# Metering side work to an allowance per weight unit in a two-layer block on one core, with the high parts of both units ahead of both low parts, and another start and end

## The chip, the cores and the metric

One core of one Trainium2 chip runs the whole program. The time is device microseconds (us) of one execution; several executions are timed and the median is given. TensorE (PE) multiplies; VectorE (DVE), ScalarE (ACT) and GpSimd (POOL) do elementwise work; SyncE (SP) issues nearly all DMAs.

## The reference, cut to what matters

Batch 1, 256 tokens, width 2048, all in fp32. Two blocks follow one another:

```
def first_block(x, mem, ...):
    h = rmsnorm(x, mix_norm);  proj = h @ w_mix_in                  # 2048 -> 7184
    y_gdn = gated_delta_rule(...conv, silu, l2norm of proj...)      # 8 heads of 128, chunks of 64,
                                                                    # a triangular solve per chunk
    y_sc  = b_gate * causal_dwconv(c_gate * h)                      # width 1024
    x = x + concat(y_gdn, y_sc) @ w_mix_out
    x = x + softmax(q k^T) v @ w_xo                                 # q from rmsnorm(x), k, v from rmsnorm(mem)
    x = x + (silu(gate) * up) @ w_ffn_down                          # gate, up = causal_dwconv(rmsnorm(x) @ w_ffn_up)
    return rmsnorm(x, final_norm)
def second_block(x, ...):
    proj = rmsnorm(x, g_pre) @ w_in
    o_mla = causal softmax attention, 8 heads, rope, low-rank q and kv;  times silu(gate)
    o_fox = causal softmax attention, 8 heads, with forget gates;        times silu(gate)
    return x + rmsnorm(concat(o_mla, o_fox) @ w_out, g_post)
```

## The kernel before

Every large weight is cut into units of 128 x 1024 (512 KB), 704 in all, which go by in one long list (`stream`). fp32 accuracy comes from two parts of each operand: a high part, rounded to the fast fp32r type, and a low part, the remainder. Unit i is loaded by SP (`load`, L335, 8 units ahead), rounded by ACT (`split_hi`, L342, into the tile `whi`, 3 units ahead, 4 buffers), and its remainder is made by DVE (`split_lo`, L349, into `wlo`, 2 units ahead, 3 buffers).

TensorE then works on the unit's 8 blocks of 128 x 128 (`blocks`): 8 high matmuls 128x512 of `whi` against a token tile that holds high and low part side by side (`x`, 2 x 256 columns), and 8 low matmuls 128x256 of `wlo` against the high part of the token tile alone. Most products (`jobB`) are jobs of two units that sum 16 blocks into one PSUM bank: high (L217) and low (L219) of the first unit, seven high, eight low and one last high (L221) of the second. There are four such banks. A job ends with `merge` (L226, L228), an ACT copy and a DVE add that bring the bank to SBUF and set it free. Products with tokens as the stationary side (`jobA`, L296 to L298: w_xv, w_fv, w_out_2) use three matmuls 128x512 per block and token half. In the last of them both token halves share the weights: some units of the second half are held back (`early`) until the sums of the first half are under way.

All else is side work in Python generators, each of which issues a few instructions and yields: squares of the inputs for the first norm (`g_first`, whose adds on POOL stand at L533 and which PE sums at L412), the gated delta rule (`g_gdn`, `g_base` for the 16x16 triangular bases at L870 and L872), convolutions after the merges (L463, L466), the memory branch (`g_mem`), attention heads (`g_xhead`, `g_head`), output gates (`p_outgate`), and the end (`g_out`). After each unit `step` advances every live generator once, whatever it issues. So the list of units, and how many generators are alive, set the order of instructions on DVE and ACT, where `split_lo` and `split_hi` stand in line with side work:

```
for i, u in enumerate(units):
    self.split_hi(i + self.LOOK_HI)
    self.split_lo(i + self.LOOK_LO)
    for h in hooks.get(id(u), ()):
        h()
    u[2](self.whi.pop(i), self.wlo.pop(i))
    ...
    self.step()
```

At the start SP issues the constants `cst` (259 KB), the first token tiles `xr0` (256 KB), the first unit `raw0` (512 KB), then the other seven token tiles with units between them; `first_x` scales each token tile (L518 on ACT, L519 on DVE) and ten warm-up matmuls on zeros (L505, 20 records in the trace) run ahead of the first weight. At the end `p_last` and `g_out` do for each token half: ACT squares (L1445), a DVE multiply by the gain (L1446), a reciprocal root in small steps, and per half four tiles of o * r + x: three on DVE (L1463) and one on ACT and POOL (L1460, L1461), then four output DMAs on SP.

## Time and profile before

| | us |
|---|---|
| median of 3 runs (lowest, highest) | 2079.64 (2078.51, 2080.05) |
| profiled execution | 2080.9 |
| its span, first to last instruction | 2079.1 |
| PE busy in the span | 2056.3 (99%) |
| DVE busy | 1484.6 (71%) |
| ACT busy | 1096.8 (53%) |
| POOL busy | 184.4 (9%) |

Spans and busy times are of the profiled execution, which took 1.26 us more than the median of the runs. Its mean granted TensorE clock was 0.996 of full speed. A matmul's record overlaps the next one's, since they are pipelined: the distance from one start to the next says how long PE needs for each.

### The profile page before, as it was taken

Reading aid. Unit: us, or ns where it says so; the run is one execution under the profiler, and the core shown is the slowest. Engines: PE = TensorE matmul, PEld = TensorE weight load, DVE = VectorE, ACT = ScalarE, POOL = GpSimd, SP = SyncE. Lnnn points to the kernel's source line nnn. Section 1 sums busy time; section 2 is a strip of 40 time slices with the busy share of each in tenths; the row PEclk is TensorE's granted clock in tenths of the full one; section 3 lists DMA queues with packets and bytes.
Section 4 is the critical chain, followed back from the end, with each engine's and each line's share of the span. In section 5 each row is a group of like instructions: output and inputs, shape, how many; then the busy total and the mean of one; then the engine's idle time right before and its main releaser. Section 6 shows DMA issues by size and latency. Waiting matters only on the chain.

```text
span 2079.1 us, 31159 instructions
## 1 busy us (share of the span) xinstructions
PE 2056.3 (99%) x11734; PEld 1802.6 (87%) x11734; DVE 1484.6 (71%) x2365; ACT 1096.8 (53%) x1751; POOL 184.4 (9%) x174
## 2 busy tenths in 40 slices
PE   8999999999999999999999999999999999999998
PEld 7888898888888898888888888888888888888886
DVE  5988679765467667777775787757779776657855
ACT  5755554644444555465543555434556655546653
POOL 2020012200001001100000000000009430000000
PEclk9999999999999999999999999999999999999999
DMA  7455446545565535555555555555546678544553
GB/s 281 161 174 192 144 152 204 174 152 193 192 225 191 171 112 188 188 189 186 193 185 192 189 187 192 186 189 192 184 156 203 210 217 226 175 157 150 196 185 102
DMA packets 136663, 381.43 MB, mean 183 GB/s; under 512 B 33600, under 2 KB 41536, under 8 KB 136512
## 3 DMA queue, kind: packets, MB, share of 16 engines
q1 hardware_dynamic: 136512, 379.44, 56.0%
q8 instruction: 92, 1.51, 0.3%
q14 instruction: 59, 0.48, 0.1%
HBM read 372.84 MB, written 5.90 MB: 182 GB/s over the span
## 4 chain that ended last, share of the span: by engine, by line
PE 95%; DVE 2%; DMA 1%; ACT 1%; issue 1%; POOL 0%; SPq 0%; DVEq 0%; POOLq 0%; ACTq 0%
PE mm L217 48%; PE mm L219 27%; PE mm L298 4%; PE mm L296 4%; PE mm L297 4%; PE mm L221 3%; DVE wlo L349 1%; POOL acc L533 0%; DMA raw<-w_mix_in 0%; PE ps L399 0%; PE ps L397 0%; PE ps L398 0%; DMA xr<-xT 0%; DVE bt L870 0%; PE ps L1370 0%
## 5 line engine op out<-in xcount | busy, mean ns | idle before, releaser
L217 PE MATMUL mm<-x,whi 128*128 128x512 f32 x4520 | 1153.6, 395 | 3.6 <-ACT whi L342 1.3
L349 DVE TENSOR_TENSOR wlo<-raw,whi 128x1024 fp32r<-128x1024 f32 (+2 forms) x704 | 859.4, 1223 | 386.3 <-PE mm L219 148.4
L217 PEld LDWEIGHTS mm<-x,whi 128*128 128x128 f32 x4520 | 830.1, 189 | 160.1 <-DVE x L519 2.8
L342 ACT CAST whi<-raw 128x1024 fp32r<-128x1024 f32 (+2 forms) x704 | 717.8, 1031 | 259.8 <-PE mm L298 104.0
L219 PEld LDWEIGHTS mm<-x,wlo 128*128 128x128 f32 x4840 | 664.1, 191 | 55.9 <-DVE wlo L349 6.4
L219 PE MATMUL mm<-x,wlo 128*128 128x256 f32 x4840 | 679.3, 283 | 5.2 <-DVE wlo L349 5.2
L226 ACT COPY mg<-mm 128x256 f32<-128x256 f32 x240 | 89.5, 373 | 462.5 <-PE mm L221 462.0
L466 DVE SCALAR_TENSOR_TENSOR cv<-pre,cst,cv 128x256 f32<-128x256 f32 x264 | 130.2, 495 | 9.7 <-ACT cv L463 1.3
L296 PE MATMUL mm<-whi,x 128*128 128x512 f32 x336 | 132.0, 393 | 0.0
L298 PE MATMUL mm<-whi,x 128*128 128x512 f32 x336 | 130.9, 389 | 0.0
L297 PE MATMUL mm<-wlo,x 128*128 128x512 f32 x336 | 130.8, 389 | 0.0
L221 PE MATMUL mm<-x,whi 128*128 128x512 f32 x320 | 126.6, 396 | 0.0
L1134 POOL TENSOR_SCALAR hf<-hf,cst 128x256 f32<-128x256 f32 x16 | 25.2, 1575 | 684.3 <-PE mm L221 683.9
L298 PEld LDWEIGHTS mm<-whi,x 128*128 128x128 f32 x336 | 63.1, 188 | 13.3
L297 PEld LDWEIGHTS mm<-wlo,x 128*128 128x128 f32 x336 | 63.1, 188 | 13.0
L228 DVE TENSOR_TENSOR ms<-mm,mg 128x256 f32<-128x256 f32 x178 | 74.3, 417 | 0.0
L296 PEld LDWEIGHTS mm<-whi,x 128*128 128x128 f32 x336 | 63.1, 188 | 12.7
L221 PEld LDWEIGHTS mm<-x,whi 128*128 128x128 f32 x320 | 61.3, 192 | 0.0
L463 ACT ACTIVATE cv<-pre,cst 128x256 f32<-128x256 f32 x120 | 60.4, 508 | 1.5 <-DVE pre L241 1.5
L447 ACT ACTIVATE x<-hf,cst 128x256 fp32r<-128x256 f32 x32 | 16.4, 513 | 81.1 <-DVE hf L1011 81.1
L241 DVE TENSOR_TENSOR pre<-ms,rb 128x256 f32<-128x256 f32 x112 | 47.6, 428 | 6.0 <-ACT rb L441 2.5
L1116 DVE TENSOR_TENSOR hf<-mm,hf 128x256 f32<-128x256 f32 x48 | 20.2, 421 | 43.2 <-PE mm L221 43.2
(344 smaller groups left out, 1229.2 us busy)
## 6 DMA issues: line engine op xcount, KB each, us to landing
raw<-w_ffn_up SPq DMA_DIRECT2D x176, 512.0 KB, 3.3
raw<-w_mix_in SPq DMA_DIRECT2D x114, 512.0 KB, 3.8
raw<-w_in SPq DMA_DIRECT2D x86, 512.0 KB, 3.4
raw<-w_ffn_down SPq DMA_DIRECT2D x80, 512.0 KB, 3.3
raw<-w_xk SPq DMA_DIRECT2D x32, 512.0 KB, 3.3
raw<-w_xv SPq DMA_DIRECT2D x32, 512.0 KB, 3.3
raw<-w_mix_out SPq DMA_DIRECT2D x32, 512.0 KB, 3.3
raw<-w_xq SPq DMA_DIRECT2D x32, 512.0 KB, 3.3
```

The lines of the kernel that those rows point to most:

```text
L217: T.matmul(ps, hi[:, c[j]], x[j].t, start=first and j == 0, stop=False)
L219: T.matmul(ps[:, 0:TOK], lo[:, c[j]], x[j].hi, start=False, stop=False)
L221: T.matmul(ps, hi[:, c[end]], x[end].t, start=first and end == 0, stop=True)
L226: self.AC.copy(t, ps[:, TOK:])
L228: self.V.tensor_tensor(out, ps[:, 0:TOK], t, ADD)
L296: self.T.matmul(ps, x.hi[:, s], hi[:, c], start=k == 0, stop=False)
L297: self.T.matmul(ps, x.hi[:, s], lo[:, c], start=False, stop=False)
L298: self.T.matmul(ps, x.lo[:, s], hi[:, c], start=False, stop=k == K - 1)
L342: self.AC.copy(hi[:, 0:F], self.raw[i][:, 0:F])
L349: self.V.tensor_tensor(lo[:, 0:F], self.raw.pop(i)[:, 0:F], fl(self.whi[i][:, 0:F]), SUB)
L463: self.AC.activation(t, pre[:, o : o + TOK], AF.Identity, scale=taps[:, 0:1])
L466: self.V.scalar_tensor_tensor(t, pre[:, o + j : o + j + TOK], taps[:, j : j + 1], t, MUL, ADD)
```

## The change

Side work is metered. `Meter` wraps the handles of DVE and ACT that generators use and adds a nominal cost for each instruction issued; the two splits of weights go around it. After each unit `step` adds an allowance (2.1 for DVE, 2.2 for ACT, never saved up), advances new generators first and then the older ones in their order, and stops as soon as either allowance is used up; who was not reached waits for a later unit. A job of two units that is not interleaved with others is "joined": its first unit issues high matmuls alone, its second its high ones, the low ones of both units, and the last high one; for that `wlo` has four buffers. At the start `raw0` is the first load on SP, and ACT issues a small DMA of 8 KB with the norm's gain and `xr0`; `cst` comes after unit 4; the first rounding of weights stands ahead of the token tiles on ACT, two token tiles are rounded on DVE, and there are 6 warm-ups in place of 10. The squares for the first norm are spread over units, half of their sums on DVE. `g_base` yields about twice as often, the memory branch starts at unit 78 in place of 100, and the last `jobA` holds back one unit more. At the end DVE does all four tiles of a half, and the second half's output DMAs alternate between SP and ACT.

```diff
-MEM_AT = 100
-WARM = 10
+MEM_AT = 78
+WARM = 6
+class Meter:
+    COST = {"scalar_tensor_tensor": 0.5, "tensor_tensor": 0.45, "tensor_reduce": 0.4, "activation": 0.45, "copy": 0.45}
+    def __getattr__(self, name):
+        self.spent += self.COST.get(name, 0.2)
+        return getattr(self.eng, name)
+class Job(list):
+    def join(self):
+        self.st["joined"] = len(self) == 2
+        return self
...
+    SPARE = (2.1, 2.2)
...
     def step(self):
-        for g in list(self.gens):
+        m = (self.V, self.AC)
+        for i in range(2):
+            self.left[i] = min(self.left[i] + self.SPARE[i], self.SPARE[i])
+        now, new, self.fresh = self.fresh + self.gens, self.fresh, []
+        self.gens += new
+        for g in now:
+            for i in range(2):
+                self.left[i] -= m[i].spent
+                m[i].spent = 0.0
+            if min(self.left) <= 0:
+                return
             try:
                 next(g)
             except StopIteration:
                 self.gens.remove(g)
-        self.gens += self.fresh
-        self.fresh = []
...
+    def blocks(self, ps, hi, lo, j0, xs, k0, n, first, last, held=()):
+        m = n - 1 if last else n
+        self.highs(ps, hi, j0, xs, k0, m, first)
+        if last:
+            self.need(xs[k0 + m])
+        for h in held:
+            self.lows(ps, *h)
+        self.lows(ps, lo, j0, xs, k0, n)
+        if last:
+            self.T.matmul(ps, hi[:, (j0 + m) * P : (j0 + m + 1) * P], xs[k0 + m].t, start=first and m == 0, stop=True)
...
                 if k0 == 0:
                     st["ps"] = self.mmbank()
-                self.blocks(st["ps"], hi, lo, 0, xs, k0, nk, k0 == 0, k0 + nk == K)
+                    if st["joined"]:
+                        self.highs(st["ps"], hi, 0, xs, 0, nk, True)
+                        st["held"] = [(lo, 0, xs, 0, nk)]
+                        return
+                self.blocks(st["ps"], hi, lo, 0, xs, k0, nk, k0 == 0, k0 + nk == K, st.pop("held", ()))
...
-                if early and n - 1 > i >= n - self.LOOK_LO - 1:
+                if early and n - 1 > i >= n - self.LOOK_LO - 2:
...
-            lo = self._t(self.wp, 1024, "wlo", self.LOOK_LO + 1, "wlo", F32R)
-            self.V.tensor_tensor(lo[:, 0:F], self.raw.pop(i)[:, 0:F], fl(self.whi[i][:, 0:F]), SUB)
+            cuts = [(j * F // parts, (j + 1) * F // parts) for j in range(parts)]
+            lo = self._t(self.wp, 1024, "wlo", self.LOOK_LO + 2, "wlo", F32R)
...
-        nc.sync.dma_start(self.cst, A["cst"])
+        nc.scalar.dma_start(self.mixg, A["cst"][:, 0:KD])
...
+        self.load(0)
+        get(0, nc.scalar)
+        for j in (1, 2, 3):
+            get(j, nc.sync)
...
+            if k in (2, 3):
+                self.V.tensor_scalar(x.hi, src[k], g, None, MUL)
+            else:
+                self.AC.activation(x.hi, src[k], AF.Identity, scale=g)
...
+        for j in range(8):
+            sqs.append(self.S("sq"))
+            self.AC.activation(sqs[j], raws[j], AF.Square)
+            if 0 < j < 4:
+                self.G.tensor_tensor(sqs[0], sqs[0], sqs[j], ADD)
+            if j > 4:
+                self.V.tensor_tensor(sqs[4], sqs[4], sqs[j], ADD)
+            yield
...
-            if spent > 1300:
+            if spent > 700:
...
-            if m == 1:
-                AC.activation(o, o, AF.Identity, scale=r)
-                G.tensor_tensor(o, o, x, ADD)
-            else:
-                V.scalar_tensor_tensor(o, o, r, x, MUL, ADD)
-        for m in (0, 2, 1, 3):
-            self.nc.sync.dma_start(self.A["out"][t * P : (t + 1) * P, m * 512 : (m + 1) * 512], self.og[t, m])
+            V.scalar_tensor_tensor(o, o, r, x, MUL, ADD)
+            q = self.nc.scalar if m % 2 and t else self.nc.sync
+            q.dma_start(self.A["out"][t * P : (t + 1) * P, m * 512 : (m + 1) * 512], o)
```

Three places show how instructions move. The first is TensorE in one job of w_ffn_up. `mm` is the job's PSUM bank, `x` a token tile, `whi` and `wlo` are the unit's two parts. Before, the first unit's low run ends, seven high matmuls of the second unit follow, and its own low run:

```order
L219 MATMUL mm_9199<-x_8361,wlo_9140 128x256
L217 MATMUL mm_9199<-x_8414,whi_9138 128x512
L217 MATMUL mm_9199<-x_8467,whi_9138 128x512
L217 MATMUL mm_9199<-x_8520,whi_9138 128x512
L217 MATMUL mm_9199<-x_8573,whi_9138 128x512
L217 MATMUL mm_9199<-x_8626,whi_9138 128x512
L217 MATMUL mm_9199<-x_8679,whi_9138 128x512
L217 MATMUL mm_9199<-x_8732,whi_9138 128x512
L219 MATMUL mm_9199<-x_8414,wlo_9168 128x256
```

Of the change, the same job at the border of its two units and at the start of its low matmuls:

```order
L250 MATMUL mm_9198<-x_8305,whi_9090 128x512
L250 MATMUL mm_9198<-x_8358,whi_9090 128x512
L250 MATMUL mm_9198<-x_8411,whi_9132 128x512
L250 MATMUL mm_9198<-x_8464,whi_9132 128x512
L250 MATMUL mm_9198<-x_8517,whi_9132 128x512
L250 MATMUL mm_9198<-x_8570,whi_9132 128x512
L250 MATMUL mm_9198<-x_8623,whi_9132 128x512
L250 MATMUL mm_9198<-x_8676,whi_9132 128x512
L250 MATMUL mm_9198<-x_8729,whi_9132 128x512
L254 MATMUL mm_9198<-x_8082,wlo_9134 128x256
L254 MATMUL mm_9198<-x_8102,wlo_9134 128x256
```

The high matmuls of two units now stand in one run of 15, and 16 low ones follow: one change from low to high inside the job is gone, the one at its last high matmul stays. 265 jobs are joined, and 566 places at which a low matmul of a weight is followed by a 128x512 one become 351.

The second place is VectorE at the end of `g_base` in the first group of heads, around the subtractions (L349 before, L403 after) on which TensorE waits. `bt` and `bw` are the scratch of the triangular base, `sch` is a value of the short convolution. Before, the last three row steps of the base stand between two subtractions:

```order
L349 TENSOR_TENSOR wlo_1739<-raw_1462,whi_1706 128x1024
L870 TENSOR_TENSOR bt_356<-bz_354,bw_355 64x169
L872 TENSOR_REDUCE bw_355<-bt_356 64x13
L870 TENSOR_TENSOR bt_356<-bz_354,bw_355 64x196
L872 TENSOR_REDUCE bw_355<-bt_356 64x14
L870 TENSOR_TENSOR bt_356<-bz_354,bw_355 64x225
L872 TENSOR_REDUCE bw_355<-bt_356 64x15
L349 TENSOR_TENSOR wlo_1772<-raw_1515,whi_1737 128x1024
```

Of the change:

```order
L403 TENSOR_TENSOR wlo_2179<-raw_1940,whi_2139 128x1024
L946 TENSOR_TENSOR bt_356<-bz_354,bw_355 64x169
L948 TENSOR_REDUCE bw_355<-bt_356 64x13
L946 TENSOR_TENSOR bt_356<-bz_354,bw_355 64x196
L948 TENSOR_REDUCE bw_355<-bt_356 64x14
L1006 TENSOR_TENSOR x_2137<-scb_1617,x_2137 128x256
L403 TENSOR_TENSOR wlo_2199<-raw_1967,whi_2177 128x1024
L274 TENSOR_TENSOR ms_2227<-mm_2183,mg_2228 128x256
L946 TENSOR_TENSOR bt_356<-bz_354,bw_355 64x225
L948 TENSOR_REDUCE bw_355<-bt_356 64x15
```

The same three steps are now on both sides of a subtraction, and that subtraction is one of a later unit.

The third place is ScalarE in w_out_2, the last weight, where the last head of the second attention (`ps` to `hf`), its gated output (`og`, cast to the token tile `x`) and the rounding of weights share the queue. Before, the copies of the last two heads and both casts stand behind the rounding of `whi_19974` and ahead of the next:

```order
L342 CAST whi_19950<-raw_19719 128x1024
L342 CAST whi_19974<-raw_19755 128x1024
L1374 COPY hf_19992<-ps_19968 128x256
L1374 COPY hf_19992<-ps_19971 128x256
L1420 CAST x_19795<-og_19812 128x256
L1420 CAST x_19869<-og_19886 128x256
L342 CAST whi_19999<-raw_19793 128x1024
```

Of the change, the last head alone, whose tile x_19844 the second of the two blocks of TensorE's unit `whi_19985` reads:

```order
L393 CAST whi_19963<-raw_19748 128x1024
L393 CAST whi_19985<-raw_19774 128x1024
L393 CAST whi_20007<-raw_19822 128x1024
L1441 COPY pT_20025<-ps_20003 128x384
L393 CAST whi_20027<-raw_19842 128x1024
L393 CAST whi_20048<-raw_19886 128x1024
L1452 COPY hf_19957<-ps_20045 128x256
L1498 CAST x_19844<-og_19869 128x256
```

The last head's copy and cast now stand behind the rounding of `whi_20048`, which takes the buffer of `whi_19963`, four units back.

## Rows read from the trace of the kernel before

**Rows 1.** TensorE's waits: what it waited for, us in total, times, longest.

```profile
PE mm L219 <- DVE wlo L349: 5.2, 3, 2.4
PE ps L412 <- POOL acc L533: 2.6, 1, 2.6
...
PE mm L217 <- ACT whi L342: 1.3, 2, 0.7
PE mm L217 <- DVE x L519: 1.2, 2, 1.0
...
PE mm L217 <- DVE x L455: 0.5, 1, 0.5
```

**Rows 2.** Stretches of half clock: busy us per engine, PEclk, DMA share, GB/s.

```profile
12.88:16.29 3.41, 3.41 (x13) 2.97 (x13) 3.41 (x8) 3.41 (x9) 0.00 (x0) 0.50 1.04 410
...
36.77:40.18 3.41, 3.41 (x13) 2.95 (x12) 0.00 (x0) 0.00 (x0) 0.00 (x0) 0.50 1.03 262
...
347.40:350.80 3.40, 3.40 (x10) 2.63 (x9) 3.37 (x5) 1.93 (x3) 1.65 (x1) 0.50 0.84 259
```

**Rows 3.** Timeline of PE after the third long wait: start, us, group.

```profile
347.36 3.58 PE L217 MATMUL mm<-x,whi 128*128 128x512 f32 x8
```

**Rows 4.** Timeline of PE: two job starts, a run of 512, a run of 256.

```profile
1010.27 1.09 PE L217 MATMUL mm<-x,whi 128*128 128x512 f32 x4
...
1038.21 2.00 PE L217 MATMUL mm<-x,whi 128*128 128x512 f32 x8
...
2010.24 0.39 PE L298 MATMUL mm<-whi,x 128*128 128x512 f32 x1
...
2013.87 0.39 PE L296 MATMUL mm<-whi,x 128*128 128x512 f32 x1
...
799.01 0.28 PE L397 MATMUL ps<-pT,th 128*128 128x256 f32 x1
...
801.76 0.28 PE L399 MATMUL ps<-pT,tl 128*128 128x256 f32 x1
```

**Rows 5.** Timeline of the start: ACT, DVE, then PE; in brackets idle before.

```profile
5.09 0.91 ACT L518 ACTIVATE x<-xr,cst 128x256 fp32r<-128x256 f32 x2 [2.85 <-DMA xr<-xT]
7.88 1.05 ACT L342 CAST whi<-raw 128x1024 fp32r<-128x1024 f32 x1 [1.87 <-DMA raw<-w_mix_in]
...
11.31 1.67 DVE L519 SCALAR_TENSOR_TENSOR x<-xr,cst,x 128x256 fp32r<-128x256 f32 x4
...
1.48 6.83 PE L505 MATMUL ps<-zero 128*128 128x256 f32 x20 [1.48 <-DVE zero L502]
8.98 0.73 PE L217 MATMUL mm<-x,whi 128*128 128x512 f32 x2 [0.67 <-ACT whi L342]
...
11.84 1.98 PE L217 MATMUL mm<-x,whi 128*128 128x512 f32 x4 [1.03 <-DVE x L519]
...
15.33 2.45 PE L217 MATMUL mm<-x,whi 128*128 128x512 f32 x8
```

**Rows 6.** Timeline of POOL: the adds of squares for the first norm.

```profile
22.93 12.30 POOL L533 TENSOR_TENSOR acc<-acc,sq 128x512 f32<-128x512 f32 x6 [0.23 <-ACT sq L532]
```

**Rows 7.** Timeline of DVE: two subtractions ahead of the wait at 168.

```profile
161.26 1.22 DVE L349 TENSOR_TENSOR wlo<-raw,whi 128x1024 fp32r<-128x1024 f32 x1
...
166.83 1.21 DVE L349 TENSOR_TENSOR wlo<-raw,whi 128x1024 fp32r<-128x1024 f32 x1
```

**Rows 8.** Timeline of DVE at the end, two groups of the last halves.

```profile
2067.78 3.08 DVE L1463 SCALAR_TENSOR_TENSOR o<-o,ry,xt 128x512 f32<-128x512 f32 x3
2070.79 0.68 DVE L1446 TENSOR_TENSOR o<-mm,gp 128x512 f32<-128x512 f32 x1
```

**Rows 9.** Timeline of the last heads: PE's values, ACT's copies and casts.

```profile
1988.71 0.59 PE L1370 MATMUL ps<-pT,val 128*128 128x256 f32 x2
...
1989.90 0.68 ACT L1374 COPY hf<-ps 128x256 f32<-128x256 f32 x2
1990.76 0.74 ACT L1420 CAST x<-og 128x256 fp32r<-128x256 f32 x2 [0.17 <-DVE og L1418]
```

More of the change, by code (lines that the diff above doesn't have):

```diff
@@ L125, in __init__ @@
         self.gens, self.fresh, self.posts = [], [], []
+        self.left = [0.0, 0.0]
         self.psfree, self.mmlive = 4, 0
@@ L205, in rel, with highs, lows @@
         self.mmlive -= 1
-    def blocks(self, ps, hi, lo, j0, xs, k0, n, first, last):
-        T, x = self.T, []
-        c = [slice((j0 + j) * P, (j0 + j + 1) * P) for j in range(n)]
-        end = n - 1 if last else n
+    def highs(self, ps, hi, j0, xs, k0, n, first):
         for j in range(n):
-            x.append(xs[k0 + j])
-            self.need(x[j])
-            if j < end:
-                T.matmul(ps, hi[:, c[j]], x[j].t, start=first and j == 0, stop=False)
+            x = xs[k0 + j]
+            self.need(x)
+            self.T.matmul(ps, hi[:, (j0 + j) * P : (j0 + j + 1) * P], x.t, start=first and j == 0, stop=False)
+    def lows(self, ps, lo, j0, xs, k0, n):
         for j in range(n):
-            T.matmul(ps[:, 0:TOK], lo[:, c[j]], x[j].hi, start=False, stop=False)
-        if end < n:
-            T.matmul(ps, hi[:, c[end]], x[end].t, start=first and end == 0, stop=True)
+            self.T.matmul(ps[:, 0:TOK], lo[:, (j0 + j) * P : (j0 + j + 1) * P], xs[k0 + j].hi,
+                          start=False, stop=False)
+    def blocks(self, ps, hi, lo, j0, xs, k0, n, first, last, held=()):
[8 more added lines that the diff above has]
+            self.T.matmul(ps, hi[:, (j0 + m) * P : (j0 + m + 1) * P], xs[k0 + m].t, start=first and m == 0, stop=True)
     def merge(self, ps, out):
@@ L255, in jobB @@
     def jobB(self, w, ui, parts, xs, post, srcs=None):
-        st, units, k0 = {}, [], 0
+        units, k0 = Job(), 0
+        st = units.st
         K = sum(parts)
@@ L327, in skew @@
         for j in jobs[m:]:
-            out += j
+            out += j.join()
         return out
@@ L499, in first_x @@
         self.AC.activation(warm, warm, AF.Identity)
-        z = self.S("zero")
+        z = self.zero = self.S("zero")
         self.V.memset(z, 0.0)
@@ L506, in first_x @@
         self.psdone()
-        for j in range(8):
-            nc.sync.dma_start(raws[j], self.A["xT"][:, j * 512 : (j + 1) * 512])
-            if j in (0, 2, 3):
-                self.load((0, 2, 3).index(j))
+        self.load(1)
+        for j in (4, 5):
+            get(j, nc.sync)
+        self.load(2)
+        for j in (6, 7):
+            get(j, nc.sync)
         for i in range(3, self.NRAW):
             self.load(i)
-            if i == 3:
+            if i == 4:
                 self.late_constants()
@@ L879, in g_groups @@
     def g_groups(self):
-        zero = self.S("zero")
-        self.G.memset(zero, 0.0)
+        zero = self.zero
         self.dA = [self.dp.tile([4 * P + 4, P], F32, name=f"dA{t}") for t in range(2)]
@@ L886, in g_groups @@
             self.nc.sync.dma_start(block_rows(self.dX[t]), r3(zero, 4))
-        zero = None
+        zero = self.zero = None
         for g in range(2):
@@ L904, in post_c @@
         def post_c(ps):
-            self.scc[f] = self.H("scc")
-            yield from self.merge(ps, self.scc[f])
+            c = self.H("scc")
+            yield from self.merge(ps, c)
+            self.scc[f] = c
         def post_h(ps):
@@ L910, in post_h @@
             yield from self.merge(ps, t)
+            while f not in self.scc:
+                yield
             pre = yield from self.pre()
@@ L1671, in build @@
         for j in fq:
-            units += j
+            units += j.join()
         for n in range(2):
@@ L1692, in build @@
             at(j[1], mk_y(n))
-            units += j
+            units += j.join()
         self.og, self.gpost = {}, []
```

45 lines of the change are left out of this document (27 added, 18 removed).

## The prediction

> **What bounds the kernel now.** I read the page first: PE is busy for 99% of the span, DVE and ACT have room on average, so only two things can move the time: the rate at which PE works, and the moments when it stands still. The list of PE's waits comes next [rows 1]: three waits for a low part made by DVE, 5.2 us in total, one of 2.6 us for a sum of squares on POOL, and small ones for ACT's rounding, for the first token tiles and for x made at L455. The granted clock by stretches is third [rows 2]: it is at half, 1.2 in place of 2.4 GHz, in three stretches of 3.4 us. The last two of them begin just after PE had stood still for 2.6 us (for POOL) and 2.4 us (the longest for DVE); in the first, at the start, PE is also still filling up. Last, the timeline gives the rate between waits [rows 4]: from 1010.27 to 1038.21 five jobs go by, 27.94 us, 5.588 each. In a straight run a 128x512 matmul takes 0.2269 from start to start (16 intervals from 2010.24 to 2013.87), a 128x256 one 0.1196 (23 from 799.01 to 801.76), which makes 16 x 0.2269 + 16 x 0.1196 = 5.544 for a job. So 0.044 us of a job is lost where one kind follows the other, and everything else is the work itself, which the change leaves as it is.
>
> **The change part by part.** The sum is made against the profiled execution, 2080.9 us.
>
> *Joined jobs.* A job has two places where a low run gives way to a high matmul, so one is worth about 0.022 us, or less if the loss depends on how long the run was. The order of the change takes 215 such places away: 215 x 0.022 = 4.7 as the upper end, zero as the lower, if the loss falls to each matmul and not to the border. I take 3.5, since joining puts small matmuls of side work at some of the new borders. Gain 3.5.
>
> *The sum of squares.* Before, six adds on POOL take 12.3 us in one piece [rows 6] and PE, in line behind them, waits 2.6 us [rows 1]. The change does three adds and a final one on POOL and three on DVE, one per unit, and PE's sum is asked for some 17 units from the start in place of about ten. A unit takes 2.79 us (half of a job), so seven units give 20 us more, against 12.3 us for all the adds even if POOL had kept them. Gain 2.6. Conversely the norm's factor comes ten units later, and merges and convolutions that wait for it pile up: this is the burst, priced below.
>
> *The waits for low parts.* The wait at 168 has its cause in [rows 7]: two subtractions that stand one behind the other start 5.57 us apart, because three merge steps of g_base, at a time when POOL works beside them, fill the gap. The unit period is 2.79 us, and a lead of two units covers one such gap only if it starts full. With the allowance of 2.1 per unit and the finer yield, a subtraction comes after each portion of side work, and the fourth buffer and the joined order let the low part come later than the high one. So I let all 5.2 us go, and put what may come back elsewhere into a term of its own. The wait of 0.6 for ACT's rounding and 0.5 for x at L455 [rows 1] come from the same bursts: gain 5.2 + 0.6 + 0.5 = 6.3. If the meter's nominal prices are too low, at the worst none of it comes.
>
> *The half clock.* Eight high matmuls in the third stretch took 3.58 us to the end of the last [rows 3], at full rate 8 x 0.2269 and 0.17 for the drain of a record, 1.99: loss 1.6. The second stretch holds 3.41 us of half rate too and cannot lose more than half of it, 1.7; PE did other short work in it, so I take 1.4. Both stood right behind waits that the terms above remove. Gain 3.0; it is zero for a stretch whose wait stays.
>
> *The start.* ACT got the first token tile at 5.09, with 515 KB issued (constants and xr0), and the first weight at 7.88, with 1027 KB [rows 5]. The change issues raw0, xr0 and 8 KB first, 776 KB by the time both are there. On a line between the two points that is 5.09 + 2.79 x 261/512 = 6.5. The first weight's rounding then starts 1.4 us earlier, or 2.8 if raw0 has the lines to itself. But PE needs eight token tiles for the first unit, and the eighth limits: DVE's group of four ends at 12.98 [rows 5], and PE goes to the next unit at 15.33, part of it at half clock. Without two roundings of weights ahead of the tiles on ACT, and with two tiles on DVE, I put the eighth tile at 11.9 and the next unit at 13.5. Gain 1.8, from 0.5 (one rounding's half) to 2.8 (the whole earlier start). Going from ten warm-ups to six shortens work that no one waits for, and that even in its old length ended at 8.31, ahead of the first weight's matmul at 8.98 [rows 5].
>
> By the Trainium skill, "DMA: Bandwidth & Descriptors", section "Issuing engines are not separate DMA queues", a transfer that ACT issues runs on the same 16 engines as SP's and interleaves with them, and only the time to issue is saved. It speaks against counting 5.09 for the first weight: with it the start would give 1.4 us there, without it 2.8. The trace of before has no large transfer from a second issuer, so no row here shows it.
>
> *The end.* One unit more held back puts six more matmuls 128x512 behind the first half's last one: it is complete 6 x 0.2269 = 1.4 us earlier, while the end of PE stays. The second half then waits on DVE: its multiply at 2070.79 stands directly behind the first half's three tiles, which took 3.08 us beside POOL's adds, 1.03 each [rows 8]. Alone the nearest operation on such a tile takes 0.68, so four take 2.7. DVE is free earlier by 1.4 + 3.08 - 2.7 = 1.8, but the multiply cannot start before PE and ACT have given it its input, which costs me 0.9 of that; the second half's own tiles give 0.35. Gain 1.2, from 0.9 to 1.5.
>
> *A new wait.* In w_out_2 the last head's copy and cast now stand on ACT behind the rounding that takes the buffer of four units back. This rounding can start only when PE has finished that unit. From there: rounding 1.05 [rows 5], then copy to cast, 1989.90 to about 1991.2 for the first of the two tiles [rows 9], 1.3; with two hand-overs of some 0.1, 2.5 us. PE has the head's own matmuls meanwhile, about 0.6 [rows 9], and three of 128x512, 0.7. It waits 2.5 - 1.3 = 1.2. The lower end is 0, when ACT's rounding gets an earlier start than I think, the upper 1.8, when the low part of x adds a DVE step. Loss 1.2.
>
> *What bursts may be left.* The late norm factor leaves convolutions of about 23 units to be caught up under the meter, beside the heads' solves, and the meter counts nominal and not real times: the three steps of g_base that filled 5.57 - 1.22 = 4.35 us between two subtractions [rows 7] count 3 x (0.45 + 0.4) = 2.55. At most this brings back the waits of before, 5.2, and a part of their half clock, at the least nothing; I take 1.0. Loss 1.0.
>
> Sum: 3.5 + 2.6 + 6.3 + 3.0 + 1.8 + 1.2 - 1.2 - 1.0 = 16.2, so 2064.7 for an execution like the profiled one. That was 1.26 above the median of its kernel, so a median of about **2063.5**.
>
> **The rivals.** *The bursts stay under the meter* and PE still waits long enough for the half clock: the waits for DVE and one stretch of half clock come back, 5.2 + 1.6 less the 1.0 counted, plus 0.6: 2070. For it speaks that 4.35 us of real time count as 2.55 in the meter; against it that one such step no longer brings two more with it, so that a gap between subtractions ends sooner. *The joined order gives nothing*, the loss being part of each matmul: 2067. Against it stands that straight runs of either kind have shown a shorter distance than a job [rows 4]. *The clock at the start:* PE's first unit was partly at half clock with ten warm-ups already [rows 2], after an idle time of 1.03 [rows 5]. With six, which would run to about 1.48 + 6.83 x 0.6 = 5.6 at the old rate, the idle time to the first weight is longer, and another stretch of 3.4 us may be at half clock: at most 1.7 more, 2065. The Trainium skill, "TensorE: Matmul & The Clock Gate", section "Part 1: The HAM clock gate (the "warmup" mystery)", says that the throttled state is the default and that activity lifts it. By that rule fewer warm-ups would make this case the likely one; the trace agrees as far as that the start has such a stretch. *Slower:* the meter starves the merges. A job's bank is free only after its merge, and with four banks PE can run three jobs, 16.8 us, ahead of it. If an empty allowance puts off merges by more than that, PE waits for a bank; spread over the 265 joined jobs, 0.08 us each is 21 us and would eat the whole gain: 2085 or more. It decides where queued side work is more than 2.1 per unit for long; DVE is 71% busy with 1.22 per unit in subtractions, which leaves some 0.9 per unit of side work on average, and that speaks against it. *The change does nothing* to the waits, which move to other units: within 0.2%. And all may go better, to 2059, if no burst is left and the last head is in time.
>
> **How the numbers follow.** The forecast has 0.52, bursts that stay 0.16 (2070), the joined order for nothing 0.10 (2067), the clock at the start 0.10 (2065), the better end 0.04 (2059), no change 0.03 and starvation 0.05. All but the last two lie below 2075.5, which is 0.2% or 4.2 us under the time before, about what a measurement of this kernel can tell from no change. So faster has 0.91, the same 0.04, slower 0.05. The range leaves out the last two, and reaches from 2058 to 2071: the lower end has the upper ends of the start (+1.0), the joined order (+1.2) and the end (+0.3), no burst (+1.0) and no wait for the last head (+1.2), 4.7 below the forecast, and 0.8 for the spread of runs; the upper end is where bursts stay, with as much.
>
> **What would show it.** In the profile of the changed kernel: no stretch of half clock after the first 20 us; the list of PE's waits without L533's successor and with under 2 us for low parts; a joined job 5.57 us from start to start in the same stage; the first run of eight low matmuls near 11.7 and the second unit at 13.5; one wait of about 1.2 us for the tile of the last head near 1990; the last group on DVE done 1.2 us closer to PE's last matmul. The forecast is wrong if waits for a PSUM bank appear, if waits for low parts are over 5 us, or if the half clock follows a wait again.

## The result and the profile after

The changed kernel takes 2092.15 us (median of 6 runs, 2088.59 to 2092.68) against 2080.19 for the kernel before: a ratio of 1.0055 (95% interval 1.0042 to 1.0068), 12 us slower where 16 us faster was forecast. The profiled execution took 2092.3 us.

The page after, its span and its engines:

```profile
span 2090.5 us, 30823 instructions
PE 2061.0 (99%) x11726; PEld 1803.0 (86%) x11726; DVE 1465.9 (70%) x2373; ACT 1091.7 (52%) x1747; POOL 206.5 (10%) x168
```

TensorE's waits after, in the form of [rows 1] (four rows of 0.7 and 0.8 us are left out):

```profile
PE ps L1438 <- DVE lg L1432: 4.4, 4, 1.5
PE mm L254 <- DVE wlo L403: 2.2, 4, 1.0
PE ps L812 <- DMA X<-dX: 2.0, 1, 2.0
PE ps L569 <- DVE zero L566: 1.5, 1, 1.5
PE ps L775 <- ACT hf L704: 1.3, 1, 1.3
PE ps L755 <- DVE A L748: 1.3, 1, 1.3
PE ps L466 <- POOL a L1210: 1.2, 1, 1.2
PE mm L250 <- DVE ms L274: 1.2, 2, 0.6
PE ps L466 <- POOL a L1211: 1.1, 1, 1.1
PE mm L347 <- ACT x L1498: 1.0, 1, 1.0
```

The waits for low parts have shrunk as foreseen, from 5.2 to 2.2 us. But before, 8.7 of 12.8 us were waits of a matmul on a weight (`mm`). Now 14.4 of 20.3 us are waits of `ps`, the small matmuls of side work, which stand in TensorE's line between the units: for logits of the heads (L1438), for a transposed copy that comes by DMA (L812), for sums on POOL (L466).

The half clock has moved too. Three stretches, as in [rows 2], 17.1 us in all where the kernel before had 10.2:

```profile
153.82:160.65 6.83, 6.83 (x27) 6.15 (x27) 4.43 (x5) 0.00 (x0) 2.56 (x2) 0.50 0.43 138
...
228.91:232.33 3.42, 3.42 (x13) 2.89 (x14) 3.31 (x6) 1.47 (x2) 0.00 (x0) 0.50 0.77 236
...
1621.55:1628.38 6.83, 6.11 (x20) 5.34 (x21) 3.55 (x7) 2.83 (x4) 2.54 (x2) 0.50 0.81 278
```

Each stands behind one of the new waits: the first 2.3 us behind it, with small side matmuls between, the other two within 1 us. To see where in the program time comes and goes, I sorted the starts of all matmuls that write `mm`; both kernels have the same 10688. The table gives the n-th start in the kernel before, and how much later (+) it comes in the others, each in its profiled execution. The runs named in it are explained below.

```
n-th weight matmul        0     128    2816    8192    9216    last
before, us              9.0    40.6   597.6  1563.4  1748.5  2068.7
changed               -1.77   -8.22   -1.28   -1.33   +5.27  +12.75
no_join               -1.38   -7.83   -5.40   -4.49   -0.47   +6.13
mirror                -1.80   -8.23   -6.35   -5.05   +0.42   +6.82
b_join                -0.08   +2.81   +1.03   -1.58   -1.10   -1.30
no_meter              -1.55   -7.71   +6.87   +4.35   +4.81   +4.71
old_order             -1.41   -7.73  +18.98  +18.08  +17.86  +23.59
no_cap                -1.67   -8.13  +17.87  +15.99  +22.65  +22.89
b_meter               -0.91   -5.76   +6.77  +11.23  +18.23  +24.76
parts                 -1.39   -7.83   -8.42   -9.14   -8.60   -8.53
late_old              -1.92   -8.39   -0.59   -2.34   -1.93   -2.03
late_cap              -1.49   -7.87   -5.64   -5.65   -5.88   -0.10
late_first            -1.82   -8.29   -3.26   -5.00   +1.78   +2.02
join_late             -1.58   -8.02   -8.89  -10.12   -9.71   -9.80
no_early_meter        -1.63   -8.00   +5.70   +3.59   +4.06   +3.96
spare3                -1.39   -7.46   +8.60   +7.32   +7.88   +7.80
```

The changed kernel wins 8.2 us by the 128th matmul and loses 6.9 of it up to the 2816th (597.6 us), gets even in the long stretch of w_ffn_up and w_ffn_down, and loses 6.6 and 7.5 in the last two columns. At the very end it wins 1.4: from the last matmul's start to the end of the span it is 10.4 us before (2079.1 - 2068.7) and 9.0 after (2090.5 - 2081.5). The sum, -8.2 + 6.9 - 0.1 + 6.6 + 7.5 - 1.4 = 11.3, is the difference of the spans, 11.4, but for rounding.

Each line of the table is one execution. Up to the 2816th, TensorE's matmuls stand in the same order in changed, late_old, late_cap and late_first, and in one other order in no_join, parts and join_late. Yet from the 128th to the 2816th the first four took 559.2 to 564.8 us, and the other three 556.1 to 559.4. So differences of a few us between two lines of this stage can be chance; the medians of the runs decide there.

Each stage splits into TensorE's waits (of over 0.15 us), what the half clock cost (half of its time), and the rest, which is matmuls at full clock:

```
n-th weight matmul   before = waits + half clock + rest    changed
128 to 2816          557.0 =   6.3 + 1.7 + 548.9           563.9 = 6.9 + 5.1 + 551.9
2816 to 8192         965.8 =   0.5 + 0.0 + 965.3           965.7 = 2.6 + 0.0 + 963.1
8192 to 9216         185.1 =   0.0 + 0.0 + 185.1           191.7 = 3.3 + 3.4 + 185.0
9216 to last         320.3 =   0.0 + 0.0 + 320.3           327.7 = 5.4 + 0.0 + 322.3
```

In the long stretch the joined order does win some 2 us, and new waits, two of them of 0.6 us for a PSUM bank, take as much.

The start after, in the order of [rows 5]:

```profile
4.35 1.04 ACT L393 CAST whi<-raw 128x1024 fp32r<-128x1024 f32 x1 [1.19 <-DMA raw<-w_mix_in]
6.13 1.71 ACT L589 ACTIVATE x<-xr,mixg 128x256 fp32r<-128x256 f32 x4 [0.73 <-DMA xr<-xT]
...
11.37 1.34 PE L254 MATMUL mm<-x,wlo 128*128 128x256 f32 x8
12.54 1.98 PE L250 MATMUL mm<-x,whi 128*128 128x512 f32 x8
```

The first weight is there at 4.35, sooner than the 6.5 I had, and the second unit starts at 12.54, 2.8 us earlier than before: the upper end of that term. No half clock falls into it in this execution. By the rule of the Trainium skill ("DMA: Bandwidth & Descriptors", "Issuing engines are not separate DMA queues"), that transfers of different issuers run on the same 16 engines and interleave, I had let the two share the lines, which gives 1.4 us. The trace agrees with the rule and not with my use of it. The token tile stood in ACT's queue behind the 8 KB of the norm's gain, 128 packets of 64 bytes from 2.34 to 3.99 us, and by the tile's own first packet at 3.89 SP's queue had moved 620 KB. From there to the tile's last packet the two did share: 256 KB by ACT's queue and some 270 by SP's.

A joined job at two starts five jobs apart, as in [rows 4]:

```profile
1003.42 3.58 PE L250 MATMUL mm<-x,whi 128*128 128x512 f32 x15
...
1031.25 3.58 PE L250 MATMUL mm<-x,whi 128*128 128x512 f32 x15
```

That is 27.83 / 5 = 5.566 us a job, 0.022 less than before, as forecast (5.57).

Now the losses. Two places early, with the DMA that the second waits for:

```profile
148.21 2.00 PE L250 MATMUL mm<-x,whi 128*128 128x512 f32 x8
151.50 0.63 PE L755 MATMUL ps<-mats,hf 128*128 128x128 f32 x4 [1.30 <-DVE A L748]
...
224.84 2.00 PE L250 MATMUL mm<-x,whi 128*128 128x512 f32 x8
228.83 1.93 PE L812 MATMUL ps<-mats,X 128*128 128x128 f32 x8 [2.00 <-DMA X<-dX]
...
223.47 0.94 SPq L804 DMA_DIRECT2D X<-dX  x2
```

In both, TensorE has only the eight high matmuls of a job's first unit, 1.8 us, between one step of the generators and the next; before, each unit had its low part too, 2.8 us. Behind each wait stands one of the half-clock stretches. Without short units these waits shrink rather than vanish (0.5 and 1.2 us in join_late, below).

Around 1620, TensorE and POOL:

```profile
1618.25 1.11 PE L254 MATMUL mm<-x,wlo 128*128 128x256 f32 x8
1620.60 0.61 PE L466 MATMUL ps<-mats,a 128*128 128x1 f32 x4 [1.24 <-POOL a L1210]
1622.27 1.01 PE L466 MATMUL ps<-mats,a 128*128 128x1 f32 x4 [1.06 <-POOL a L1211]
...
1618.77 1.78 POOL L1210 TENSOR_TENSOR a<-a,s 128x256 f32<-128x256 f32 x1 [0.29 <-ACT s L1204]
1620.52 1.70 POOL L1211 TENSOR_TENSOR a<-a,s 128x256 f32<-128x256 f32 x1
```

The sums for two norms stand in TensorE's line one unit behind the step that gives POOL its last adds.

Among the heads, one of the four waits for logits, on DVE and PE:

```profile
1931.07 0.42 DVE L274 TENSOR_TENSOR ms<-mm,mg 128x256 f32<-128x256 f32 x1 [0.56 <-ACT mg L272]
...
1932.07 0.55 DVE L1432 TENSOR_SCALAR lg<-lg,sm 128x128 f32<-128x128 f32 x2
...
1932.50 0.61 PE L1438 MATMUL ps<-mats,lg 128*128 128x128 f32 x3 [1.50 <-DVE lg L1432]
```

The logits' scaling stands on DVE behind a merge that itself waits for ACT; the transposition on PE, one unit later in the program, comes before it is done.

### The profile page after: what moved, and what is told of

It reads as the page before. It is cut to its first block, busy times and chain, and to the rows that moved or that the text cites. A ratio compares the mean times of both kernels' runs of the same rounds, so it can differ in the third digit from the quotient of the medians.

```text
span 2090.5 us, 30823 instructions
## 1 busy us (share of the span) xinstructions
PE 2061.0 (99%) x11726; PEld 1803.0 (86%) x11726; DVE 1465.9 (70%) x2373; ACT 1091.7 (52%) x1747; POOL 206.5 (10%) x168
## 4 chain that ended last, share of the span: by engine, by line
PE 92%; DVE 4%; ACT 2%; issue 1%; DMA 0%; POOL 0%; DVEq 0%; ACTq 0%; SPq 0%; POOLq 0%
PE mm L250 46%; PE mm L254 26%; PE mm L347 4%; PE mm L349 4%; PE mm L348 4%; PE mm L267 3%; DVE wlo L403 2%; DVE cv L520 0%; PE ps L453 0%; PE ps L451 0%; PE ps L452 0%; PE ps L812 0%; PE ps L823 0%; PE ps L840 0%; ACT L1493 0%
## 5 line engine op out<-in xcount | busy, mean ns | idle before, releaser
L250 PE MATMUL mm<-x,whi 128*128 128x512 f32 x4520 | 1114.6, 394 | 2.8 <-DVE ms L274 1.2
L250 PEld LDWEIGHTS mm<-x,whi 128*128 128x128 f32 x4520 | 843.9, 189 | 171.9 <-DVE x L590 3.2
L403 DVE TENSOR_TENSOR wlo<-raw,whi 128x1024 fp32r<-128x1024 f32 (+2 forms) x705 | 863.1, 1242 | 106.3 <-ACT whi L393 90.4
L254 PEld LDWEIGHTS mm<-x,wlo 128*128 128x128 f32 x4840 | 630.1, 192 | 33.0 <-DVE wlo L403 4.4
L254 PE MATMUL mm<-x,wlo 128*128 128x256 f32 x4840 | 639.9, 283 | 2.4 <-DVE wlo L403 2.2
L349 PE MATMUL mm<-whi,x 128*128 128x512 f32 x336 | 131.0, 390 | 0.0
L267 PE MATMUL mm<-x,whi 128*128 128x512 f32 x320 | 126.7, 396 | 0.0
L1212 POOL TENSOR_SCALAR hf<-hf,cst 128x256 f32<-128x256 f32 x16 | 15.9, 995 | 681.8 <-ACT a L1205 681.8
L349 PEld LDWEIGHTS mm<-whi,x 128*128 128x128 f32 x336 | 63.1, 188 | 13.7 <-DVE x L1500 0.2
L1184 ACT CAST x<-cv 128x256 fp32r<-128x256 f32 x44 | 17.9, 407 | 101.0 <-DVE cv L1182 101.0
L267 PEld LDWEIGHTS mm<-x,whi 128*128 128x128 f32 x320 | 61.4, 192 | 0.0
```

The costliest lines, as they stand in the source:

```text
L250: self.T.matmul(ps, hi[:, (j0 + j) * P : (j0 + j + 1) * P], x.t, start=first and j == 0, stop=False)
L254: self.T.matmul(ps[:, 0:TOK], lo[:, (j0 + j) * P : (j0 + j + 1) * P], xs[k0 + j].hi, start=False, stop=False)
L267: self.T.matmul(ps, hi[:, (j0 + m) * P : (j0 + m + 1) * P], xs[k0 + m].t, start=first and m == 0, stop=True)
L349: self.T.matmul(ps, x.lo[:, s], hi[:, c], start=False, stop=k == K - 1)
L403: self.nc.vector.tensor_tensor(lo[:, c[0] : c[1]], r[:, c[0] : c[1]], h[:, c[0] : c[1]], SUB)
```

## The experiments

Fourteen kernels were run, each timed beside the kernel before, whose medians were 2079.93 to 2080.76 us. Ratios are to it, with 95% intervals.

| run | us | ratio |
|---|---|---|
| no_join | 2084.01 | 1.0018 (1.0009 to 1.0027) |
| no_meter | 2085.02 | 1.0023 (1.0014 to 1.0032) |
| mirror | 2085.48 | 1.0027 (1.0018 to 1.0036) |
| b_join | 2078.38 | 0.9993 (0.9985 to 1.0002) |
| old_order | 2102.80 | 1.0110 (1.0097 to 1.0124) |
| no_cap | 2101.42 | 1.0100 (1.0085 to 1.0116) |
| b_meter | 2100.79 | 1.0105 (1.0091 to 1.0119) |
| parts | 2071.20 | 0.9959 (0.9947 to 0.9972) |
| late_old | 2075.09 | 0.9975 (0.9967 to 0.9984) |
| late_cap | 2081.89 | 1.0011 (1.0002 to 1.0020) |
| late_first | 2081.39 | 0.9998 (0.9989 to 1.0007) |
| join_late | 2070.65 | 0.9952 (0.9940 to 0.9965) |
| no_early_meter | 2084.01 | 1.0019 (1.0010 to 1.0028) |
| spare3 | 2084.95 | 1.0024 (1.0015 to 1.0033) |

**First: joined jobs or the meter?** no_join takes the joined order out:

```diff
     def join(self):
-        self.st["joined"] = len(self) == 2
         return self
```

> The changed kernel with no job joined: both units of a job again do their high and then their low matmuls; everything else as changed. Theory J (the joined order makes the first unit of a job 1.8 us and the second 3.7 us long for TensorE, and side matmuls that come after the short unit wait for VectorE, ScalarE or a DMA that had 2.8 us before): most of the new waits behind runs of eight high matmuls go, 10 to 14 us with their half clock, and 4 to 5 us of the joined order's own gain is lost: 2082 to 2087. Theory M (the meter puts side work off until TensorE waits for it): the waits stay and the joined gain is lost, 2096 to 2098.

It came out at 2084.0, in theory J's range. In the table, undoing the order is worth 4.1 us by the 2816th matmul, costs 1.0 in the long stretch behind it, and is worth 2.6 and 0.9 in the last two stages. But most of the late losses stay: +4.0 and +6.6 from 8192 on. So J explains a part only.

no_meter goes back to the old step (every generator once per unit, new ones after it) and `MEM_AT = 100`:

> The changed kernel with the step of the kernel before, that advances every generator once per unit, and the memory branch at unit 100 as before; joined jobs and all else as changed. Theory J: the short first units remain and with them the waits, 2088 to 2096. Theory M: the waits of side matmuls go, 2074 to 2080.

Measured 2085.0, between the two theories, because it does both. It loses 14.6 us up to 2816, where weights wait again (10.4 us for low parts, 4.3 for x of DVE, 2.4 for ACT's rounding), and 0.4 after 8192. So the new step, together with the earlier memory branch, pays early and costs late. A single number would have hidden that; the table by stages shows it.

mirror keeps as few changes from low to high, with even units: the first does high then low, the second low then high.

```diff
-                    if st["joined"]:
-                        self.highs(st["ps"], hi, 0, xs, 0, nk, True)
-                        st["held"] = [(lo, 0, xs, 0, nk)]
-                        return
+                elif st["joined"]:
...
+                    self.lows(ps, lo, 0, xs, k0, nk)
+                    self.highs(ps, hi, 0, xs, k0, e, False)
...
+                    return
```

> The changed kernel, its joined jobs in another order: the first unit does high and then low matmuls, the second its low ones first and then its high ones. A job has as few changes from low to high as in the joined order, but both units last 2.8 us. Theory J: the joined gain of 4 to 5 us stays and the waits go, 2078 to 2083. Theory M: as the changed kernel, 2090 to 2094.

2085.5: neither. The early loss is 1.9 in place of 6.9, as J says, but the second unit now starts with its low part, and this wait took the place of the others, ten times; in the early stage side matmuls wait only 1.6 us for ACT and 0.2 for the DMA:

```profile
PE mm L254 <- DVE wlo L407: 9.4, 10, 2.0
```

b_join adds joined jobs and the fourth buffer to the kernel before:

> The kernel before with joined jobs and the fourth wlo buffer alone. Theory J: 4 to 5 us gained by the order, 8 to 12 lost in waits behind short units: 2083 to 2088. Theory M: the gain alone, 2074 to 2077.

2078.4, a little above theory M's range: here theory J failed. With the old step, joined jobs lose nothing up to 2816 (1.8 gained after the start) and win 4.1 in all after the 128th matmul; 2.8 are lost at the start, where in this execution the half clock lasts 6.8 us twice in place of 3.4 [rows 2]. Whether the joined order causes that or it is chance is open: the eleven times lie between 2075.6 and 2081.3. So early the short unit costs only together with the new step.

**Second: which half of the new step?** old_order keeps the allowance but advances old generators first, new ones from the next unit on (memory branch at 100):

```diff
-        now, new, self.fresh = self.fresh + self.gens, self.fresh, []
-        self.gens += new
-        for g in now:
+        for g in list(self.gens):
...
-                return
+                break
...
+        self.gens += self.fresh
+        self.fresh = []
```

> The changed kernel with its allowance, but generators advanced in the order of before: old ones first, and one that a unit has made waits for the next unit's step; the memory branch at unit 100. Theory F (new generators first takes away a unit of lead between work on VectorE or POOL and the side matmul that reads it): the waits for POOL near 1620 and for the heads' logits after 1920 go, 2078 to 2084. Theory A (the allowance itself puts work off until TensorE waits for it): 2089 to 2094.

2102.8, outside both, by an early loss that I had only as a rival: merges stand last in line, get nothing from the allowance, and TensorE waits for a PSUM bank. The first row of its waits:

```profile
PE mm L250 <- DVE ms L274: 16.0, 6, 8.3
```

Late, it is clear: nothing lost between 8192 and 9216 (-0.2), 5.7 after it. no_cap has the new order with `SPARE = (1000.0, 1000.0)`, and the memory branch at 100:

> The changed kernel with an allowance that never runs out, new generators first as changed; the memory branch at unit 100. Theory F: the late waits of the changed kernel stay, and the early ones of the run without the meter come to them, 2092 to 2100. Theory A: as the run without the meter, 2083 to 2087.

2101.4, just above theory F's range, but again mostly by the early stage (26 us from 128 to 2816, with waits of 7.7 us for ACT's rounding, 5.8 for a value of the delta rule and 5.2 for low parts). Late it is the reverse of old_order: 6.7 lost between 8192 and 9216, 0.2 after. So both theories hold, each in one stage. b_meter adds the new step alone to the kernel before:

> The kernel before with the new step alone (meter, allowance, new generators first). If the new step costs what it seems to cost late in the changed kernel, also without joined jobs: some 10 us lost after 1560 and up to 5 gained before 600, 2083 to 2088. If it only costs together with joined jobs: 2075 to 2079.

2100.8, above both ranges: 7.0 and 6.5 are lost in the last two stages without any joined job (its profiled execution took 2105.7, 4.9 over its median). Early, the longest wait is 10.8 us for a tile of the memory branch. I take it that under an allowance unit 100 is too late a start for that branch, which is 78 in the change; no run tests it alone.

parts puts each piece where it had paid: joined jobs in w_ffn_up alone, the old step from unit 330 on.

```diff
+        if self.at_unit >= 330:
+            return self.step_all()
...
-            out += j.join()
+            out += j.join() if join else j
```

> The changed kernel with each part where it paid: joined jobs in w_ffn_up alone, where there is next to no side work, the new step up to unit 330, the old step after it. Sum of the differences read so far by stages: 5.4 gained by 600 us, 1.7 in w_ffn_up, 1.4 at the end, nothing lost after 1560: 2069 to 2074. If the late losses have another cause than step and joined jobs, 2080 or more.

2071.2, as summed, 8.9 under the kernel before.

**Third: the late causes one by one.** late_old is the changed kernel with the old step from unit 330:

> The changed kernel, all jobs joined, with the old step from unit 330 on (from about 850 us). By the stages read so far the late losses of 6.4 (around 1600) and 7.5 (after 1750) go and the early ones stay: 2076 to 2080. Against the run of parts it differs by joined jobs elsewhere: 4 to 7 lost by the short units before 600 us, 1.5 to 2.5 gained after it. If joined jobs cost nothing before 600, it comes out at 2069 to 2070.

2075.1, just under the range. Nothing is lost after 8192, and the early loss is there (-8.4 to -0.6). late_cap has the allowance from there on, in the old order; late_first the new order without an allowance:

> As late_old, but from unit 330 the allowance holds, with the old order of generators. If the allowance is what costs after 1750 (two heads that went in step are pulled apart, and TensorE waits for their logits) and nothing else: about 6 over late_old, all of it after 1750, nothing around 1600: 2082 to 2086. If it needs the new order too: as late_old.

> As late_old, but from unit 330 new generators come first, without an allowance. If the order is what costs around 1600 (the sums for the two norms asked of TensorE a unit before POOL has added): 6 to 7 over late_old, all of it between 1560 and 1660, nothing after 1750: 2082 to 2087. If it needs the allowance too: as late_old.

2081.9 and 2081.4, each just under its range: they cost 6.8 and 6.3 over late_old. In the table late_first loses 6.8 between 8192 and 9216 alone, and late_cap 5.8 in the last column. Against late_old it also loses 1.7 in the long stretch, which I had not expected: there TensorE waits twice 0.6 us for a bank, as in the changed kernel. (That late_cap's line ends only 1.9 over late_old's is the early stage, where both run the same program.) Behind the 2816th the changed kernel loses 15.5 us against late_old; late_cap has 7.0 of it and late_first 6.7, and 1.8 is in neither alone. The waits of late_first between 1560 and 1750 are those of the changed kernel, beside one of 1.0 us for a low part in both:

```profile
PE ps L479 <- POOL a L1223: 1.2, 1, 1.2
PE ps L479 <- POOL a L1224: 1.1, 1, 1.1
```

What the allowance does to the heads is seen on ACT, where each change between the exponential of the heads and the gates' activation loads a table. From 1911 to 1980 late_old has 6 such loads in three pairs:

```profile
1911.74 1.28 ACT L1441 ACT_TABLE_LOAD   x1
1916.12 1.28 ACT L1506 ACT_TABLE_LOAD   x1
1943.38 1.28 ACT L1441 ACT_TABLE_LOAD   x1
1947.76 1.28 ACT L1506 ACT_TABLE_LOAD   x1
```

Two heads go in step and share a pair. In late_cap, from 1905 to 1976, there are ten, one pair for nearly every head, and ten as well in the changed kernel from 1916 to 1988:

```profile
1905.93 1.28 ACT L1450 ACT_TABLE_LOAD   x1
1908.22 1.28 ACT L1515 ACT_TABLE_LOAD   x1
1918.07 1.28 ACT L1450 ACT_TABLE_LOAD   x1
1920.36 1.28 ACT L1515 ACT_TABLE_LOAD   x1
```

After 1750 TensorE waits 4.0 us in late_cap, for logits, for the last head's tile and for a copy of a transposition. The other 1.8 of its 5.8 us are neither wait nor half clock: the last stage's matmuls at full clock take 322.0 us in place of 320.2 in late_old. I put that down to more changes between weight and side matmuls, since the heads no longer share them, but did not test it. join_late is parts with joined jobs in w_ffn_down, w_in_2 and the gates too:

> The run of parts with joined jobs also in w_ffn_down, w_in_2 and the gates, not before. Some 75 more jobs of 0.02 us each, 1.5 gained, if side work there has enough lead with the old step: 2069 to 2070.5. If short units cost there too, over 2072.

2070.65, the best of all, 10.1 us under the kernel before. Each against the kernel before beside it, join_late gains 1.2 us more than parts; the intervals of the two ratios overlap, though the last column agrees (-9.80 against -8.53).

**Fourth: did the meter do anything for the weights?** no_early_meter is join_late with the old step throughout and, as a second edit, the memory branch at 100:

> As join_late, but with the old step from the first unit, and the memory branch at unit 100 as before: no allowance anywhere, no joined jobs ahead of w_ffn_up. If the meter is what keeps bursts of side work off the weights before 600 us: waits for low parts and for ScalarE's roundings of 8 to 15 us come back there, 2079 to 2086. If it only moves waits about: within 3 us of join_late, 2068 to 2074.

2084.0, all of it before 2816. Its waits from 41 to 600 us:

```profile
PE mm L266 <- DVE wlo L415: 11.3, 6, 4.1
PE mm L262 <- DVE x L522: 4.3, 2, 2.3
PE mm L262 <- ACT whi L405: 1.4, 1, 1.4
```

In the same stretch join_late waits 1.3 us for low parts and not at all for the other two. So the meter does what was said of it, unless it is the branch's start; spare3, which keeps that start at 78, speaks for the meter. The waits that come back are over twice the old 5.2 us; that the later norm of the new start makes a larger burst would explain it, but is not shown. spare3 raises the early allowance to 3.0 and 3.1:

> As join_late, with an early allowance of 3.0 and 3.1 in place of 2.1 and 2.2. If the waits of side matmuls left before 600 us (5 us in all) come from work put off by the allowance, they shrink while waits for low parts grow little: 2067 to 2070. If the allowance is what keeps VectorE ahead of the weights, waits for low parts grow by 2 us or more: 2072 to 2077.

2084.95, far above both ranges: it falls back altogether, with 10.7 us of waits for low parts in that stretch. Somewhere between an allowance of 2.1 and one of 3.0 lies a step of 14 us.

## Why the prediction was wrong

The terms that were read from a row held. The start: forecast 1.8, second unit 2.8 earlier. The sum of squares: POOL's wait is gone. The rate of a joined job: 5.566 as forecast, and 4.1 us in b_join behind the start, against 3.5. The end: 1.4 against 1.2. The last head's tile: a wait of 1.0 us against 1.2. Waits for low parts went with the meter, by more than their old size (no_early_meter). And the half clock did vanish from its old places, but more of it came in new ones, so that the gain of 3.0 became a loss of 3.4 (half of 17.1 - 10.2).

The step that failed is the last of the sum, "What bursts may be left ... I take 1.0". I priced there only what side work does to the weights, that is lateness of DVE's subtractions. I did not price what reordering does to the matmuls of side work itself. These stand in TensorE's line between two units, and what covers their operands is the work of one unit between two steps. The order shown before the prediction had it in view: eight high matmuls with no low ones behind them are a unit of 1.8 us in place of 2.8. I read it as a rate and not as a lead. It cost in three places, 4.4, 6.8 and 5.8 us, where that term had 1.0; a fourth cost, 1.7 us, is a small case of the merges that starve, which I had among the rivals:

- *Before 597.6 us* short units and the new step together. late_old and join_late differ only in the joined jobs ahead of w_ffn_up, and their medians lie 4.4 us apart: 2075.09 (2072.77 to 2077.86) and 2070.65 (2069.77 to 2071.78). In the profiled executions, from the 128th to the 2816th matmul, the four with early joined jobs and the new step (changed, late_old, late_cap, late_first) took 562.5 us on the mean and the three with the new step alone (no_join, parts, join_late) 557.3. Of these 5.2 us, 2.8 are waits (7.4 against 4.6), 1.4 half clock and 0.9 the matmuls at full clock. Joined jobs without the new step cost nothing (b_join 555.2, before 557.0). That it is the lead of 1.8 us, mirror supports: its units are even, and of the 6.2 us that side matmuls wait in the changed kernel there, 1.8 are left; but its weights wait instead (558.8 in all). The waits of late_old, then those of join_late, from 41 to 600 us:

```profile
PE ps L825 <- DMA X<-dX: 3.8, 4, 2.6
PE ps L768 <- DVE A L761: 1.3, 1, 1.3
PE ps L788 <- ACT hf L717: 1.3, 1, 1.3
...
PE ps L788 <- ACT hf L717: 1.6, 1, 1.6
PE mm L266 <- DVE wlo L415: 1.3, 3, 0.6
PE ps L825 <- DMA X<-dX: 1.2, 2, 1.0
PE ps L768 <- DVE A L761: 0.5, 1, 0.5
```

- *From 597.6 to 1563 us* the allowance: 1.7 us in late_cap against late_old, of which 1.2 are two waits for a bank. It takes back what the joined order wins there.
- *Between 1563 and 1748 us* new generators first: late_first isolates it, 6.8 us. The sums are asked of TensorE 2.8 us too soon, it waits 1.2 and 1.1 for POOL and 1.0 for a low part, and 6.8 us of half clock follow, which cost 3.4. I had taken this stretch as free of change but for joined jobs.
- *After 1748 us* the allowance: late_cap isolates 5.8 us of the changed kernel's 7.5. It pulls apart pairs of heads that went in step.

So the sentence "everything else is the work itself, which the change leaves as it is" was wrong in what it left out: in the kernel before TensorE waits 0.5 us in all after 600 us, which I took for a stretch where nothing could be lost. It was one where the old step gave every side matmul its lead.

The term for low parts, 5.2, was right in its mechanism, and its gain is in join_late: from 128 to 2816 it is at 556.1 us, 0.9 under the kernel before. Waits of 1.6, 1.3, 1.2 and 0.5 us (a copy on ACT, low parts, a transfer, a product on DVE) have come in place of the old 6.3, no half clock costs the old 1.7, but the matmuls at full clock take 551.4 us in place of 548.9. Why these 4.6 us of waits and the 2.5 us are left without joined jobs stays open. With the old step (no_meter, no_early_meter) no side matmul waits over 0.4 us there, so the waits belong to the new step; a larger allowance (spare3) made the weights wait. So with the four costs above taken out join_late gains 10.1 us, not the forecast 16.2.

Of the rivals, the bursts that stay were the nearest in kind, yet it was not the weights that waited. The clock at the start did not come in the changed kernel's profiled execution, but it came in six of the thirteen profiled executions with six warm-ups, 3.41 us long from 9 to 10 us on, and cost little: these six were 7.8 us ahead at the 128th matmul on the mean, the others 8.2. The starved merges did not decide the changed kernel (two waits of 0.6 for a bank) but were real in old_order, 16.0 us, where the generators' order let them starve. The chances listed for a faster kernel add up to 0.92, not 0.91, which changes nothing. Two of my signs that would show the forecast wrong came: the half clock followed waits again, and waits for a bank appeared.

## What to carry to other kernels

Where a bottleneck engine runs small work of its own between its large pieces, that work's operands live on the length of the piece ahead of it: an edit that makes pieces uneven, or that asks for the small work a step sooner, is to be priced as lost lead, also in stretches that show no wait now. A limit on side work pays where side work comes in bursts, and costs where generators went in step; the place is found by a table of time against the bottleneck's own progress, stage by stage, which two partial edits then confirm. And a stretch without waits is not proof of slack.

## What the hardware showed that I had not expected

The granted clock fell to half for 6.83 us, from 153.82, after a wait of only 1.30 us that was followed by some 3 us of small side matmuls, where the kernel before had a wait of 1.86 us at 168 with none behind it. And the same matmuls in the same order, with the same wait of 1.3 us, do not always bring it: at this place late_old and late_first had 3.41 us of half clock and late_cap none. Without short units, behind a wait of 0.5 us, no_join had 6.83 us and parts and join_late none. So how much half clock follows such a wait differs between executions, and a single profile does not price it.

And 8 KB stood ahead of 256 KB: the gain's 128 packets of 64 bytes took ACT's queue from 2.34 to 3.99 us, and the first token tile behind them could be used only at 6.13, 1.8 us after the first weight of 512 KB on SP's queue.
